# A two-block transformer layer on one core: index projections moved ahead of the convolution's, six taps moved from VectorE to ScalarE, one weight unit split

## The chip, the cores and the metric

One NeuronCore of one Trainium2 chip. The metric is the device time of one execution in microseconds. The profile of this kernel names its engines PE (TensorE, with PEld for its weight loads), DVE (VectorE), ACT (ScalarE), POOL (GpSimd) and SP (SyncE, which issues the loads).

## What is computed

Two transformer blocks on a sequence of 256 tokens and a width of 1024, in fp32. The first is a hybrid layer (three kinds of attention, a 3-tap convolution, a feed-forward part). The change lies in the second block, of which this matters:

```python
n = _rmsnorm(h, norm_mix_g)
z = n @ w_in
c_a, c_g, q, k, v, qi, ki, wi, gc_logit, ga_logit = _split_cols(z, IN_SIZES)
...
u = c_a * sigmoid(c_g)
u = conv31(u) + conv_b                       # 31 taps, causal, each channel by itself
y_conv = silu(_layernorm(u, ln_g, ln_b)) @ w_conv_out
...
logits = einsum('bqhd,bsd->bqhs', qi, ki) * IDX_DIM ** -0.5
score = einsum('bqh,bqhs->bqs', wi, relu(logits))       # causal; the 64 best keys of each query are kept
y_attn = masked_attention(q, k, v, top_k(score)) @ w_attn_out
h = h + (g_conv * y_conv + g_attn * y_attn) @ w_mix_out
```

## The kernel before, in words

**Weight units.** Every projection is cut into units of 512 inputs by 512 outputs (128 x 2048 numbers, 1 MB), 151 in all, in the fixed order of the list `order`; `_pack` lays the weights out in the same order. A unit goes through three steps. SP loads it into one of three buffers `wr`. ACT copies it to `wh`, rounded to the type fp32r (L123), and DVE writes the rest `wr - wh` to `wl` (L126), each as two halves of 128x1024. PE multiplies three times (`mm3`, L263 to L265: high by high, high by low, low by high), 48 matmuls of 256 columns a unit. A unit whose index is in `NATIVE` is not split: PE multiplies the raw fp32 numbers (L292, or L347 where tokens are the output's rows), and neither ACT nor DVE works on it. Three split units can be held (`SPLIT_BUFS`).

**Second block, units 70 to 104.** The input is `xs2` (tiles `xnh`, raw `xn`). The groups come in this order: for half 0 of the channels the convolution's gate `tg` (70, 71) and value `ca` (72, 73); the index queries `qi` (74, 75); the small unit `kiwi` (76); for half 1 `tg` (77, 78) and `ca` (79, 80); then q (81 to 84), k (85 to 88), v (89 to 92), the two gates `gc`, `ga` (93 to 100), and the attention's output product (101 to 104). The evacuation of `ca` makes `u` on DVE (`gated`, L221).

**Side work.** Two generators run beside the groups. At two points in each unit `pump()` lets each go one step, and its instructions stand in the engines' lists from there on.

- `conv()` waits until `u` of a half exists and then applies 31 taps. Tap 0 is four ACT instructions (L1136, with the bias). Of the others, those with `d % 5 < 4` go by ACT: four multiplications into a scratch tile `cp` (L1141), then one addition into `y` over the four channel groups on DVE (L1142). Those with `d % 5 == 4` go by DVE alone, as four multiply-and-add instructions (L1145). `CONV_RATE = (5, 4)` means four pauses for five taps. When both halves are done, DVE sums `y` over the channels (L1152 to L1156) and PE multiplies the sum by ones for the mean (L1159): the start of the layer norm, at whose end the convolution's output product can begin.
- `attention2()` starts when `qi` and `kiwi` exist: index logits on PE (L1060), a ReLU on ACT (L1062), the weighted sum on DVE (L1065), then eight rounds of `max` and `match_replace` on DVE for each half of the queries (L1072, L1073). It goes on with softmax attention once q, k and v are there (L1091 on PE, L1093 to L1103 on DVE and ACT, L1019 and L1032 on PE).

PE's instructions stand in the order of the program. Those of the other engines are ordered once, when the kernel is built. On every engine an instruction runs only after the one ahead of it.

Of the kernel before, what the change touches and what calls it, by code (L numbers as in the profile page):

```python
# [9 lines left out]
F32 = mybir.dt.float32  # L10
F32R = mybir.dt.float32r
AF = mybir.ActivationFunctionType
# [4 lines left out]
T = 256  # L17
# [121 lines left out]

RAW_BUFS = 3  # L140
LOAD_AHEAD = 2
NATIVE = (81, 85, 89, 97)
SPLIT_BUFS = 3
AHEAD = 3
H_BUFS = 24
CONV_RATE = (5, 4)
CONV_ACT = (4, 5)
WARM = 13
LAG = 3
# [11 lines left out]
def hybrid_conformer_kernel(ctx, tc, stop, dbg, xT, memT, wall, wtok, wkiwi, wcmp, par_d, cst_d, gfin_d, out):  # L161
    nc = tc.nc
    V, A, G, P = nc.vector, nc.scalar, nc.gpsimd, nc.tensor
# [4 lines left out]
    psm = ctx.enter_context(tc.tile_pool(name="psm", bufs=4, space=bass.MemoryType.PSUM))  # L168
    pss = ctx.enter_context(tc.tile_pool(name="pss", bufs=3, space=bass.MemoryType.PSUM))
    pso = ctx.enter_context(tc.tile_pool(name="pso", bufs=1, space=bass.MemoryType.PSUM))  # L170

    order = ["main"] * 4 + ["tok"] * 2 + ["main"] * 70 + ["kiwi"] + ["main"] * 74
    for i in NATIVE:
        order[i] = "nat"
    W = Stream(tc, ctx, wall, wtok, wkiwi, order, AHEAD)
# [10 lines left out]
    def H4(dt=F32, name="h"):  # L186
        return half.tile([128, 4, T], dt, name=name, tag="H")

    def S(shape, name, bufs=None, dt=F32):
        return sm.tile(shape, dt, name=name, tag=name, bufs=bufs) if bufs else sm.tile(shape, dt, name=name, tag=name)  # L190
# [20 lines left out]
    def plain(ps):  # L211

        return ps.rearrange("p n (a s) -> p n s a", s=2)

    def v4(ap):
        return ap.rearrange("p n (s a) -> p n s a", s=2)
# [6 lines left out]
    def v3(ap):  # L223
        return ap.rearrange("p (s a) -> p s a", s=2)
# [16 lines left out]
    def pump(n=1):  # L241
        for _ in range(n):
            now = [f for k, f in later if k == 0]
            later[:] = [(k - 1, f) for k, f in later if k]
            for f in now:
                f()
            for g in list(side):
                step(g)
# [5 lines left out]
    def start(gen, urgent=None):  # L254
        side.append((gen, URGENT if urgent is None else urgent))
        return side[-1]

    ALL8 = list(range(8))

    def mm3(ps_ap, wh, wl, xh, xl, first, last):  # L260
        ps_ap = ps_ap.rearrange("p (a s) -> p a s", s=2)
        xh, xl = turns(xh), turns(xl)
        P.matmul(out=ps_ap, lhsT=wh, rhs=xh, start=first, stop=False, skip_group_check=True)  # L263
        P.matmul(out=ps_ap, lhsT=wh, rhs=xl, start=False, stop=False, skip_group_check=True)  # L264
        P.matmul(out=ps_ap, lhsT=wl, rhs=xh, start=False, stop=last, skip_group_check=True)  # L265
# [114 lines left out]
    def group(act, kts, evac, kmajor=False):  # L380
        prod([Feat(act, kts, evac, kmajor)])
# [96 lines left out]
    with tc.manual_schedule(engines=MANUAL):  # L478
# [505 lines left out]
        xs2 = HL("xnh", raws=xn)  # L984
# [142 lines left out]
        def conv():  # L1127
            cnt = 0
            for hf in range(2):
                while ("u", hf) not in done:  # L1130
                    yield
                for d in range(31):
                    w = [par[:, wco + 8 * (30 - d) + 4 * hf + i:wco + 8 * (30 - d) + 4 * hf + i + 1] for i in range(4)]
                    if d == 0:
                        for i in range(4):
                            A.activation(out=y[hf][:, i], in_=u[hf][:, i], func=AF.Identity, scale=w[i],  # L1136
                                         bias=par[:, cbo + 4 * hf + i:cbo + 4 * hf + i + 1])
                    elif d % CONV_ACT[1] < CONV_ACT[0]:
                        p = H4(name="cp")
                        for i in range(4):  # L1140
                            A.activation(out=p[:, i, 0:T - d], in_=u[hf][:, i, 0:T - d], func=AF.Copy, scale=w[i])  # L1141
                        V.tensor_tensor(y[hf][:, :, d:T], y[hf][:, :, d:T], p[:, :, 0:T - d], op=ALU.add)  # L1142
                    else:
                        for i in range(4):
                            V.scalar_tensor_tensor(out=y[hf][:, i, d:T], in0=u[hf][:, i, 0:T - d], scalar=w[i],  # L1145
                                                   in1=y[hf][:, i, d:T], op0=ALU.mult, op1=ALU.add)
                    cnt += 1
                    if cnt * CONV_RATE[1] // CONV_RATE[0] != (cnt - 1) * CONV_RATE[1] // CONV_RATE[0]:
                        yield
                if hf == 0:  # L1150
                    s = H4(name="ys")
                    V.tensor_tensor(s[:, 0:2], y[0][:, 0:2], y[0][:, 2:4], op=ALU.add)  # L1152
                else:
                    V.tensor_tensor(s[:, 2:4], y[1][:, 0:2], y[1][:, 2:4], op=ALU.add)
                    V.tensor_tensor(s[:, 0:2], s[:, 0:2], s[:, 2:4], op=ALU.add)
                    V.tensor_tensor(s[:, 0], s[:, 0], s[:, 1], op=ALU.add)  # L1156
            yield
            ps = PS()
            P.matmul(out=ps[:, 0:T], lhsT=ones, rhs=s[:, 0])  # L1159
            mu = S([128, T], "rb", 4)  # L1160
            V.tensor_scalar(mu, ps[:, 0:T], 1.0 / D, None, op0=ALU.mult)
            sqs = []
            for hf in range(2):
                V.tensor_tensor(y[hf], y[hf], bc(mu, 4), op=ALU.subtract)
                sq = H4(name="sq")
                A.activation(out=sq, in_=y[hf], func=AF.Square)
                sqs.append(sq)
            yield
            var = fold(sqs)
            yield  # L1170
            yield
            ps = col_stats(var)
            yield
            r = rstd_col(ps, D, "rln")
            dg = col_diag(r)
            yield
            ps = diag_bcast(dg)
            rb = S([128, T], "rb", 4)
            A.activation(out=rb, in_=ps, func=AF.Copy)
            for hf in range(2):  # L1180
                t = H4(name="th")
                V.tensor_tensor(y[hf], y[hf], bc(rb, 4), op=ALU.mult)
                for i in range(4):
                    k = 4 * hf + i
                    A.activation(out=at(y, k), in_=at(y, k), func=AF.Identity, scale=par[:, lgo + k:lgo + k + 1],
                                 bias=par[:, lbo + k:lbo + k + 1])
                A.activation(out=t, in_=y[hf], func=AF.Tanh, scale=0.5)
                V.scalar_tensor_tensor(out=y[hf], in0=t, scalar=1.0, in1=y[hf], op0=ALU.add, op1=ALU.mult)
                split_into(ss_, y[hf], 4, 4 * hf, scale=0.5)

        cv = start(conv(), CONV_URGENT)

        for hf in range(2):
            tg = H4(name="tg")

            def ev_cg(ps, o, n):
                A.activation(out=v4(tg[:, o:o + n]), in_=ps, func=AF.Tanh, scale=0.5)

            def ev_ca(ps, o, n):
                gated(u[hf][:, o:o + n], tg[:, o:o + n], ps)  # L1200
                if o == 2:
                    done.add(("u", hf))

            group(xs2, ALL8, ev_cg)
            group(xs2, ALL8, ev_ca)
            if hf == 1:
                break

            qi = H4(name="qi")

            def ev_qi(ps, o, n):
                A.activation(out=v4(qi[:, o:o + n]), in_=ps, func=AF.Copy)

            group(xs2, ALL8, ev_qi)
            kiwi = S([128, T], "rb", 4)
            ps = psm.tile([128, 2, T], F32, name="m", tag="m")
            wh, wl = W.next()
            for k in range(8):
                sl = slice(128 * k, 128 * k + 128)
                mm3(ps[:, 0], wh[:, sl], wl[:, sl], xs2.hi(k), xs2.lo(k), k == 0, k == 7)  # L1220
            A.activation(out=v3(kiwi), in_=plain(ps)[:, 0], func=AF.Copy)
            pump()
            at2 = start(attention2())

        for dst in (q2, k2):
            for hf in range(2):
# [143 lines left out]
        for hf in range(2):  # L1370
            sl = slice(512 * hf, 512 * hf + 512)
# [35 lines left out]
def _units(w, pairs=0):  # L1407

    K, N = w.shape
    g = w.reshape(K // 512, 4, 128, N // 512, 512).transpose(3, 0, 2, 1, 4).reshape(N // 512, K // 512, 128, 2048)  # L1410
    a = g[:2 * pairs].reshape(pairs, 2, K // 512, 128, 2048).transpose(0, 2, 1, 3, 4)
    return np.concatenate([a.reshape(-1, 128, 2048), g[2 * pairs:].reshape(-1, 128, 2048)])
# [12 lines left out]
def _pack(inputs):  # L1425
# [12 lines left out]
    wkv = f["wx_kv_2"][0]  # L1438
    units += [_units(wkv[:, :512])]
    sl = lambda a, n: w2[:, a:a + n]  # L1440
    for h in range(2):
        units += [_units(sl(1024 + 512 * h, 512)), _units(sl(512 * h, 512))]
        if h == 0:
            units += [_units(sl(5120, 512))]
    units += [_units(sl(2048, 2048)), _turned(_units(sl(4096, 1024))), _units(sl(5704, 2048))]
    units += [_units(f["w_attn_out_2"][0]), _units(f["w_conv_out_2"][0], 1), _units(f["w_mix_out_2"][0], 1)]
    xq, xv = _units(f["wx_q_2"][0]), _turned(_units(wkv[:, 512:]))
# [72 lines left out]
```

## Time and profile before

| | |
|---|---|
| median of 3 runs | 895.7 us (895.48 to 896.13) |
| the profiled execution | 895.34 us, its span 893.6 us |
| PE, PEld busy | 881.4, 851.9 us |
| DVE, ACT busy | 659.9, 545.6 us |
| granted TensorE clock | 0.999 |

The span reaches from the first to the last instruction; 1.74 us of the profiled execution lie around it. A busy time is the union of an engine's instructions. Since one matmul begins before the last has ended, PE counts as busy all along while it is fed. In a timeline a row gives start, duration, engine, line, operation, tiles and count, and in brackets the idle time ahead of it with what ended it.

### The profile page before, as it was taken

How to read it: one execution, taken by the hardware profiler on the slowest of the kernel's cores; microseconds unless marked ns; L12 is line 12 of the kernel's file. 1: busy time of each engine (PE TensorE's matmuls, PEld its weight loads, DVE VectorE, ACT ScalarE, POOL GpSimd, SP SyncE). 2: the span in 40 equal slices, each digit the busy share in tenths (PEclk: the TensorE clock that was granted, in tenths of full speed). 3: DMA queues.
4: the chain of work that ended last, by engine and by line, in shares of the span. 5: the costliest groups of instructions: out<-in, count | busy, mean ns of one | idle time of the engine just before them, and what ended most of it. 6: DMA issues, size and time to landing. Idle time of an engine off the chain costs nothing.

```text
span 893.6 us, 17269 instructions
## 1 busy us (share of the span) xinstructions
PE 881.4 (99%) x7240; PEld 851.9 (95%) x7240; DVE 659.9 (74%) x1037; ACT 545.6 (61%) x925; POOL 17.8 (2%) x21
## 2 busy tenths in 40 slices
PE   8999999999999999999999999999999999999996
PEld 8999999999999999999998989999999999998885
DVE  6678899457786675648699999997787777665542
ACT  7634667444575564435697799977566657564432
POOL 0111000000000000000000000000000000000000
PEclk9999999999999999999999999999999999999999
DMA  8844523555555576554553356354665265555541
GB/s 306 313 167 151 211 100 137 170 205 193 189 190 189 194 247 218 191 189 143 193 207 103 138 194 231 124 193 153 208 252 201 95 217 189 191 201 214 192 142 48
DMA packets 25566, 165.01 MB, mean 185 GB/s; under 512 B 2960, under 2 KB 3600, under 8 KB 6928
## 3 DMA queue, kind: packets, MB, share of 16 engines
q1 hardware_dynamic: 25056, 163.37, 51.8%
q8 instruction: 57, 0.93, 0.4%
q10 hardware_dynamic: 432, 0.53, 0.2%
q14 instruction: 21, 0.17, 0.1%
HBM read 162.58 MB, written 1.05 MB: 183 GB/s over the span
## 4 chain that ended last, share of the span: by engine, by line
PE 81%; DVE 11%; ACT 4%; issue 2%; DMA 2%; POOLq 0%; POOL 0%; DVEq 0%; ACTq 0%
PE m L263 22%; PE m L264 22%; PE m L265 21%; PE m L350 3%; PE m L351 3%; PE m L352 3%; DVE wl L126 3%; DVE y L1142 3%; ACT cp L1141 2%; DMA wr<-in_wall_dram 1%; DVE y L1145 1%; ACT wh L123 1%; PE o L780 1%; PE s L764 1%; DVE acc L1073 1%
## 5 line engine op out<-in xcount | busy, mean ns | idle before, releaser
L126 DVE TENSOR_TENSOR wl<-wr,wh 128x1024 fp32r<-128x1024 f32 (+2 forms) x300 | 350.0, 1190 | 155.4 <-ACT wh L123 155.0
L123 ACT ACTIVATE wh<-wr 128x1024 fp32r<-128x1024 f32 (+2 forms) x300 | 298.7, 1029 | 202.6 <-PE m L264 99.6
L263 PE MATMUL m<-xh,wh 128*128 128x256 f32 x384 | 108.3, 282 | 0.6 <-ACT xh L518 0.6
L264 PE MATMUL m<-xh,wh 128*128 128x256 f32 x384 | 106.0, 276 | 0.9 <-DVE xh L520 0.9
L263 PE MATMUL m<-xnh,wh 128*128 128x256 f32 x376 | 106.6, 283 | 0.0
L265 PE MATMUL m<-xh,wl 128*128 128x256 f32 x384 | 105.6, 275 | 0.0
L264 PE MATMUL m<-xnh,wh 128*128 128x256 f32 x376 | 103.4, 275 | 0.0
L265 PE MATMUL m<-xnh,wl 128*128 128x256 f32 x376 | 103.4, 275 | 0.0
L1141 ACT ACTIVATE cp<-u,par 128x255 f32<-128x255 f32 (+23 forms) x192 | 78.8, 490 | 0.0
L263 PEld LDWEIGHTS m<-xh,wh 128*128 128x128 f32 x384 | 73.6, 192 | 2.6 <-issue 1.4
L264 PEld LDWEIGHTS m<-xh,wh 128*128 128x128 f32 x384 | 73.7, 192 | 1.7 <-DVE xh L520 1.7
L265 PEld LDWEIGHTS m<-xh,wl 128*128 128x128 f32 x384 | 73.7, 192 | 0.0
L264 PEld LDWEIGHTS m<-xnh,wh 128*128 128x128 f32 x376 | 72.2, 192 | 0.7 <-issue 0.5
L263 PEld LDWEIGHTS m<-xnh,wh 128*128 128x128 f32 x376 | 72.2, 192 | 0.7 <-issue 0.5
L265 PEld LDWEIGHTS m<-xnh,wl 128*128 128x128 f32 x376 | 72.2, 192 | 0.0
L263 PE MATMUL m<-x5h,wh 128*128 128x256 f32 x256 | 70.8, 277 | 0.0
L263 PE MATMUL m<-fh,wh 128*128 128x256 f32 x256 | 70.6, 276 | 0.0
L263 PE MATMUL m<-hh,wh 128*128 128x256 f32 x256 | 70.6, 276 | 0.0
L265 PE MATMUL m<-x5h,wl 128*128 128x256 f32 x256 | 70.4, 275 | 0.0
L264 PE MATMUL m<-fh,wh 128*128 128x256 f32 x256 | 70.4, 275 | 0.0
L265 PE MATMUL m<-fh,wl 128*128 128x256 f32 x256 | 70.4, 275 | 0.0
L264 PE MATMUL m<-hh,wh 128*128 128x256 f32 x256 | 70.4, 275 | 0.0
(380 smaller groups left out, 2323.0 us busy)
## 6 DMA issues: line engine op xcount, KB each, us to landing
wr<-in_wall_dram SPq DMA_DIRECT2D x145, 1024.0 KB, 4.9
wr<-in_wall_dram SPq DMA_DIRECT2D x4, 512.0 KB, 9.0
mem<-in_memT_dram SPq DMA_DIRECT2D x4, 512.0 KB, 6.0
wr<-in_wtok_dram SPq DMA_DIRECT2D x2, 560.0 KB, 5.1
wr<-in_wall_dram SPq DMA_DIRECT2D x4, 256.0 KB, 4.8
wck<-in_wcmp_dram SPq DMA_DIRECT2D x2, 512.0 KB, 5.9
cst<-in_cst_dram SPq DMA_DIRECT2D x1, 776.0 KB, 10.6
x<-in_xT_dram SPq DMA_DIRECT2D x2, 256.0 KB, 4.3
```

What stands on the lines that cost most here:

```text
L123: self.nc.scalar.activation(out=hi[:, sl], in_=raw[:, sl], func=AF.Copy)
L126: self.nc.vector.tensor_sub(lo[:, sl], raw[:, sl], hi[:, sl].bitcast(F32))
L263: P.matmul(out=ps_ap, lhsT=wh, rhs=xh, start=first, stop=False, skip_group_check=True)
L264: P.matmul(out=ps_ap, lhsT=wh, rhs=xl, start=False, stop=False, skip_group_check=True)
L265: P.matmul(out=ps_ap, lhsT=wl, rhs=xh, start=False, stop=last, skip_group_check=True)
L350: P.matmul(out=o, lhsT=xh, rhs=wh[:, w], start=first, stop=False)
L351: P.matmul(out=o, lhsT=xh, rhs=wl[:, w], start=False, stop=False)
L352: P.matmul(out=o, lhsT=xl, rhs=wh[:, w], start=False, stop=last)
L764: P.transpose(out=psv[:, br, b], in_=pr[:, br, b * 128:b * 128 + 128], identity=ident)
L780: P.matmul(out=po[64 * g:64 * g + 64, 0:128], lhsT=vtok[:, b, c0:c0 + 64], rhs=pts[g][:, br, b], start=False, stop=(br == 1 and b == nb - ...
L1141: A.activation(out=p[:, i, 0:T - d], in_=u[hf][:, i, 0:T - d], func=AF.Copy, scale=w[i])
L1142: V.tensor_tensor(y[hf][:, :, d:T], y[hf][:, :, d:T], p[:, :, 0:T - d], op=ALU.add)
```

## The change

The groups `qi` and `kiwi`, and with them the start of `attention2()`, come ahead of both halves of `tg` and `ca`: `qi` is now units 70 and 71, `kiwi` 72, `tg` and `ca` of half 0 are 73 to 76, those of half 1 stay 77 to 80, and all behind them keeps its place. The list `order` and `_pack` follow. `conv()` is started after `kiwi` rather than before the groups. In half 0 all 30 taps behind tap 0 go by ACT and DVE's addition; in half 1 six still go by DVE alone. `CONV_RATE` becomes (7, 5). Unit 89, the first of v, leaves `NATIVE` and is split like the others.

```diff
--- before.py
+++ after.py
@@ -139,11 +139,11 @@
 
 RAW_BUFS = 3
 LOAD_AHEAD = 2
-NATIVE = (81, 85, 89, 97)
+NATIVE = (81, 85, 97)
 SPLIT_BUFS = 3
 AHEAD = 3
 H_BUFS = 24
-CONV_RATE = (5, 4)
+CONV_RATE = (7, 5)
 CONV_ACT = (4, 5)
 WARM = 13
 LAG = 3
@@ -169,7 +169,7 @@
     pss = ctx.enter_context(tc.tile_pool(name="pss", bufs=3, space=bass.MemoryType.PSUM))
     pso = ctx.enter_context(tc.tile_pool(name="pso", bufs=1, space=bass.MemoryType.PSUM))
 
-    order = ["main"] * 4 + ["tok"] * 2 + ["main"] * 70 + ["kiwi"] + ["main"] * 74
+    order = ["main"] * 4 + ["tok"] * 2 + ["main"] * 66 + ["kiwi"] + ["main"] * 78
     for i in NATIVE:
         order[i] = "nat"
     W = Stream(tc, ctx, wall, wtok, wkiwi, order, AHEAD)
@@ -1135,7 +1135,7 @@
                         for i in range(4):
                             A.activation(out=y[hf][:, i], in_=u[hf][:, i], func=AF.Identity, scale=w[i],
                                          bias=par[:, cbo + 4 * hf + i:cbo + 4 * hf + i + 1])
-                    elif d % CONV_ACT[1] < CONV_ACT[0]:
+                    elif hf == 0 or d % CONV_ACT[1] < CONV_ACT[0]:
                         p = H4(name="cp")
                         for i in range(4):
                             A.activation(out=p[:, i, 0:T - d], in_=u[hf][:, i, 0:T - d], func=AF.Copy, scale=w[i])
@@ -1188,6 +1188,23 @@
                 V.scalar_tensor_tensor(out=y[hf], in0=t, scalar=1.0, in1=y[hf], op0=ALU.add, op1=ALU.mult)
                 split_into(ss_, y[hf], 4, 4 * hf, scale=0.5)
 
+
+        qi = H4(name="qi")
+
+        def ev_qi(ps, o, n):
+            A.activation(out=v4(qi[:, o:o + n]), in_=ps, func=AF.Copy)
+
+        group(xs2, ALL8, ev_qi)
+        kiwi = S([128, T], "rb", 4)
+        ps = psm.tile([128, 2, T], F32, name="m", tag="m")
+        wh, wl = W.next()
+        for k in range(8):
+            sl = slice(128 * k, 128 * k + 128)
+            mm3(ps[:, 0], wh[:, sl], wl[:, sl], xs2.hi(k), xs2.lo(k), k == 0, k == 7)
+        A.activation(out=v3(kiwi), in_=plain(ps)[:, 0], func=AF.Copy)
+        pump()
+        at2 = start(attention2())
+
         cv = start(conv(), CONV_URGENT)
 
         for hf in range(2):
@@ -1203,24 +1220,6 @@
 
             group(xs2, ALL8, ev_cg)
             group(xs2, ALL8, ev_ca)
-            if hf == 1:
-                break
-
-            qi = H4(name="qi")
-
-            def ev_qi(ps, o, n):
-                A.activation(out=v4(qi[:, o:o + n]), in_=ps, func=AF.Copy)
-
-            group(xs2, ALL8, ev_qi)
-            kiwi = S([128, T], "rb", 4)
-            ps = psm.tile([128, 2, T], F32, name="m", tag="m")
-            wh, wl = W.next()
-            for k in range(8):
-                sl = slice(128 * k, 128 * k + 128)
-                mm3(ps[:, 0], wh[:, sl], wl[:, sl], xs2.hi(k), xs2.lo(k), k == 0, k == 7)
-            A.activation(out=v3(kiwi), in_=plain(ps)[:, 0], func=AF.Copy)
-            pump()
-            at2 = start(attention2())
 
         for dst in (q2, k2):
             for hf in range(2):
@@ -1438,10 +1437,9 @@
     wkv = f["wx_kv_2"][0]
     units += [_units(wkv[:, :512])]
     sl = lambda a, n: w2[:, a:a + n]
+    units += [_units(sl(5120, 512))]
     for h in range(2):
         units += [_units(sl(1024 + 512 * h, 512)), _units(sl(512 * h, 512))]
-        if h == 0:
-            units += [_units(sl(5120, 512))]
     units += [_units(sl(2048, 2048)), _turned(_units(sl(4096, 1024))), _units(sl(5704, 2048))]
     units += [_units(f["w_attn_out_2"][0]), _units(f["w_conv_out_2"][0], 1), _units(f["w_mix_out_2"][0], 1)]
     xq, xv = _units(f["wx_q_2"][0]), _turned(_units(wkv[:, 512:]))
```

Three places show how the instructions move. The names: `tg`, `u`, `y`, `cp`, `ys` belong to the convolution; `kid` and `pr` with L1062 to the index; `wh` and `wl` are a unit's two parts; `xnh` the input; `pt`, `ah` and `ga` belong to attention and gates.

ACT's list where the convolution starts, before (from the last split of unit 73 on):

```order
L1197 ACTIVATE tg<-m 128x512
L123 ACTIVATE wh<-wr 128x1024
L1197 ACTIVATE tg<-m 128x512
L123 ACTIVATE wh<-wr 128x1024 x3
L1136 ACTIVATE y<-u,par 128x256 x2
L1141 ACTIVATE cp<-u,par 128x255 x2
L1141 ACTIVATE cp<-u,par 128x254
```

and in the changed kernel:

```order
L1050 ACTIVATE kid<-s 64x256 x2
L123 ACTIVATE wh<-wr 128x1024
L1062 ACTIVATE pr<-s 128x2x128
...
L1062 ACTIVATE pr<-s 128x2x128
L123 ACTIVATE wh<-wr 128x1024 x2
L1062 ACTIVATE pr<-s 128x512 x2
L1136 ACTIVATE y<-u,par 128x256
L1141 ACTIVATE cp<-u,par 128x255
L1141 ACTIVATE cp<-u,par 128x254
```

Tap 0 (L1136) stood ahead of all index work; now `kid` and six of the eight ReLUs stand ahead of it, and the splits up to unit 78.

ACT's list at the convolution's end, before:

```order
L1141 ACTIVATE cp<-u,par 128x226
L1037 ACTIVATE ah<-o 128x2x128
L1141 ACTIVATE cp<-u,par 128x226 x3
L123 ACTIVATE wh<-wr 128x1024
L1021 ACTIVATE pt<-s 128x512
L1244 ACTIVATE ga<-m,par 128x256
L1037 ACTIVATE ah<-s 128x2x128
L1244 ACTIVATE ga<-m,par 128x256
```

and now:

```order
L1141 ACTIVATE cp<-u,par 128x228 x4
L123 ACTIVATE wh<-wr 128x1024 x2
L1021 ACTIVATE pt<-s 128x512
L1243 ACTIVATE ga<-m,par 128x256
L1037 ACTIVATE ah<-o 128x2x128
L1037 ACTIVATE ah<-s 128x2x128
L1243 ACTIVATE ga<-m,par 128x256
L1141 ACTIVATE cp<-u,par 128x226 x4
L1243 ACTIVATE ga<-m,par 128x256 x2
L123 ACTIVATE wh<-wr 128x1024
```

The last tap's multiplications (128x226) stand behind one more `pt` and `ah`; the split behind them is in both the first half of unit 101. From the first L1136 to the last L1141 the list before holds 192 `cp`, 41 halves of splits (units 76 to 100, the small unit counted as one half), 8 ReLUs, 2 `qi`, 1 `kiwi` copy and 2 `kid`; now it holds 216 `cp`, 38 halves (units 79 to 100) and 2 ReLUs.

DVE's list from the last addition to the layer norm, before:

```order
L1142 TENSOR_TENSOR y<-y,cp 128x4x226
L1154 TENSOR_TENSOR ys<-y 128x512
L126 TENSOR_TENSOR wl<-wr,wh 128x1024
L1038 TENSOR_TENSOR ah<-s,ah 128x2x128
L1155 TENSOR_TENSOR ys<-ys 128x512
L1156 TENSOR_TENSOR ys<-ys 128x256
L126 TENSOR_TENSOR wl<-wr,wh 128x1024
```

and now:

```order
L1142 TENSOR_TENSOR y<-y,cp 128x4x226
L126 TENSOR_TENSOR wl<-wr,wh 128x1024
L1038 TENSOR_TENSOR ah<-o,ah 128x2x128
L1154 TENSOR_TENSOR ys<-y 128x512
L126 TENSOR_TENSOR wl<-wr,wh 128x1024
L1155 TENSOR_TENSOR ys<-ys 128x512
L1156 TENSOR_TENSOR ys<-ys 128x256
```

Both halves of unit 101 now stand between the last addition and the sum over channels, where one stood. On PE, L1159 stays where it was, behind the first half of unit 99.

## Rows read from the trace of the kernel before

**Rows 1.** The page: busy us (share of the span) xinstructions of each engine.

```profile
PE 881.4 (99%) x7240; PEld 851.9 (95%) x7240; DVE 659.9 (74%) x1037; ACT 545.6 (61%) x925; POOL 17.8 (2%) x21
```

**Rows 2.** Windows of 10 us: length, PE, PEld, DVE, ACT, POOL busy, clock, DMA share, GB/s.

```profile
470.00:480.00 10.00, 10.00 (x69) 8.41 (x69) 10.00 (x33) 7.65 (x14) 0.00 (x0) 1.00 0.16 47
...
530.00:540.00 10.00, 10.00 (x42) 7.66 (x41) 9.79 (x12) 10.00 (x21) 0.00 (x0) 1.00 0.65 250
```

**Rows 3.** Timeline of PE where the layer norm's first matmul waits.

```profile
597.25 0.28 PE L265 MATMUL m<-xnh,wl 128*128 128x256 f32 x1
598.66 0.67 PE L1159 MATMUL s<-ys,ones 128*128 128x256 f32 x2 [1.14 <-DVE ys L1156]
```

**Rows 4.** Timeline of DVE at the same place, from the last addition on.

```profile
594.17 1.09 DVE L1142 TENSOR_TENSOR y<-y,cp 128x904 f32<-128x904 f32 x1
595.30 0.69 DVE L1154 TENSOR_TENSOR ys<-y 128x512 f32<-128x512 f32 x1
595.91 1.22 DVE L126 TENSOR_TENSOR wl<-wr,wh 128x1024 fp32r<-128x1024 f32 x1
597.04 0.42 DVE L1038 TENSOR_TENSOR ah<-s,ah 128x256 fp32r<-128x256 f32 x1
597.38 0.68 DVE L1155 TENSOR_TENSOR ys<-ys 128x512 f32<-128x512 f32 x1
598.09 0.42 DVE L1156 TENSOR_TENSOR ys<-ys 128x256 f32<-128x256 f32 x1
```

**Rows 5.** Window from tap 0 to ACT's last multiplication; columns as in rows 2.

```profile
437.19:593.02 155.83, 155.07 (x1138) 143.57 (x1137) 148.77 (x264) 144.32 (x323) 0.00 (x0) 1.00 0.46 166
```

**Rows 6.** ACT's longest wait in that window: us in total, times, longest.

```profile
ACT wh L123 <- DMA wr<-in_wall_dram: 5.5, 2, 3.9
```

**Rows 7.** ACT's timeline: starts of neighbours give what each instruction takes.

```profile
437.19 1.09 ACT L1136 ACTIVATE y<-u,par 128x256 f32<-128x256 f32 x2 [1.78 <-DVE u L221]
...
444.98 1.99 ACT L123 ACTIVATE wh<-wr 128x1024 fp32r<-128x1024 f32 x2
446.87 0.61 ACT L1212 ACTIVATE qi<-m 128x512 f32<-128x512 f32 x1
447.37 2.86 ACT L1141 ACTIVATE cp<-u,par 128x251 f32<-128x251 f32 x7
450.13 0.58 ACT L1212 ACTIVATE qi<-m 128x512 f32<-128x512 f32 x1
...
457.02 0.76 ACT L1050 ACTIVATE kid<-s 64x256 f32<-64x256 f32 x2
...
460.08 0.39 ACT L1062 ACTIVATE pr<-s 128x256 f32<-128x256 f32 x1
460.36 1.06 ACT L123 ACTIVATE wh<-wr 128x1024 fp32r<-128x1024 f32 x1
```

**Rows 8.** PE's timeline: unit 70's first matmul, then index matmuls between units.

```profile
417.19 0.28 PE L263 MATMUL m<-xnh,wh 128*128 128x256 f32 x1
...
454.71 0.60 PE L1046 MATMUL s<-rb,cst 128*128 128x256 f32 x2
...
455.51 0.36 PE L263 MATMUL m<-xnh,wh 128*128 128x256 f32 x1
...
458.27 0.60 PE L1060 MATMUL s<-kid,qi 128*128 128x256 f32 x2
458.52 0.46 PE L263 MATMUL m<-xnh,wh 128*128 128x256 f32 x1
```

**Rows 9.** PE's timeline at native unit 89 and the unit behind it.

```profile
525.48 7.03 PE L347 MATMUL m<-wr,xn 128*128 128x512 f32 x16
531.95 0.78 PE L350 MATMUL m<-wh,xnh 128*128 128x512 f32 x1
```

**Rows 10.** DVE by line from 441 to 599 us: count, busy us, mean ns, idle before.

```profile
L1142 DVE TENSOR_TENSOR y<-y,cp 128x1020 f32<-128x1020 f32 (+23 forms) x48 | 55.6, 1159 | 5.0 <-ACT cp L1141 3.7
...
L1145 DVE SCALAR_TENSOR_TENSOR y<-u,par,y 128x252 f32<-128x252 f32 (+5 forms) x48 | 20.4, 463 | 0.0
```

## The prediction

> **What bounds the kernel now.** I read the page first. PE is busy for 99% of the span and its weight loads for 95%; DVE and ACT stand at 74% and 61% [rows 1]. Over the whole kernel this is a TensorE kernel, and a change to the other engines should be nearly free.
>
> The shares are means over stages, so next come the windows of 10 us in the stage that is edited, about 437 to 599 us. There DVE and ACT are nearly full: at 470 us DVE 10.00 of 10 and ACT 7.65, at 530 us 9.79 and 10.00 [rows 2]. PE is still fed, because the splits of its weights stand among the convolution's instructions in both lists.
>
> Third, PE's timeline where the two sides meet. L1159, the layer norm's first matmul, needs every tap of the convolution. PE was done with the matmuls ahead of it at about 597.4 us (the last begins at 597.25, and they begin 0.11 apart), and began L1159 at 598.66, held by DVE's `ys` [rows 3]. This is the place to watch: PE works in order, so whatever makes the convolution later is paid here in full. The convolution was 1.1 us late already.
>
> Fourth, what the convolution's end comes from. DVE's last addition began at 594.17 [rows 4], right behind ACT's last multiplications, which ended at 593.02. From tap 0 at 437.19 to there ACT was busy for 144.32 us and idle for 155.83 - 144.32 = 11.5 us [rows 5]. The longest wait in it was for loads, 5.5 us in two pieces [rows 6]. So ACT has 11.5 us of room in the window, which is what the change uses.
>
> **The change, part by part.** *Order.* PE has the same units up to 80, in another order. It gets later to the place that starts the convolution: half way through the second unit of `ca`, where the first `u` is made. In matmuls from the start of unit 70 that was number 168 (three and a half units of 48), and is now 288 (`qi` 96, the small unit 24, `tg` 96, `ca` 72). From 417.19 to 454.71 PE took 336 matmuls, 0.1117 us each [rows 8]. So the place was at 417.19 + 168 x 0.1117 = 435.95, and tap 0 began 1.24 us behind it, at 437.19 [rows 7]. Now it comes at 417.19 + 288 x 0.1117 = 449.4, plus the index matmuls that have moved ahead of it: the block at 454.71, 0.80 us, and five of L1060, four of 0.25 (458.27 to 458.52) and one of twice the columns, about 0.5 [rows 8]; together 451.7. With the same 1.24 us tap 0 starts at 452.9, **15.7 us later**. Before, ACT used those 15.7 us mostly for the convolution. L1159 does not move on PE, so the start is later and the due time is not.
>
> *ACT's work from tap 0 to the last multiplication.* I start from the 144.3 us of rows 5 and count what the lists hold there, with prices from neighbours in ACT's timeline [rows 7]:
> - 24 more multiplications (six taps, four each): seven take 447.37 to 450.13, 0.394 each; +9.5.
> - Splits: 38 halves for 41. Two of unit 89 come in, those of 76 to 78 now stand ahead. Two halves take 444.98 to 446.87, 0.945 each; -2.8.
> - Two `qi` copies (446.87 to 447.37, 0.5 each), -1.0; the small copy and two `kid` (0.76 for the pair), -1.0.
> - Six of eight ReLUs: four small (460.08 to 460.36, 0.28), two with the columns of a `qi` copy, 0.5; -2.1.
> - One `pt` and one `ah` more stand ahead of the last tap; priced as the large and small ReLU, +0.8.
>
> Sum: 147.7 us. With no idle time at all ACT ends the last tap at 452.9 + 147.7 = **600.6**, against 593.02 before. The room of 11.5 us does not help: it lay inside a window that has lost 15.7 us at its front.
>
> *Idle time of ACT in the new window.* It can be nothing, or as before, 11.5 us. I take nothing: ACT waited before where it ran ahead of PE (an evacuation not yet there) or of the loads, and it is now behind both. The other end counts for the range.
>
> *From ACT's last tap to L1159.* Before: 598.66 - 593.02 = 5.6 us. Now both halves of unit 101 stand on DVE between the last addition and the last sum, and their `wh` stands on ACT behind the last tap. So: two `ga` (about 0.4 each, an estimate from the small multiplications) and one half split on ACT, 0.8 + 0.95; then on DVE `wl` 1.13, `ah` 0.34, `ys` 0.61, `wl` 1.13, `ys` 0.71 and 0.57 to L1159 [rows 4]; 6.2 us. L1159 starts at 600.6 + 6.2 = 606.8, **8.1 us later** than before.
>
> *DVE.* A tap by L1145 cost 4 x 20.4 / 48 = 1.7 us, an addition by L1142 55.6 / 48 = 1.16 [rows 10]. Six taps save 3.2 us, unit 89's `wl` costs 2 x 1.13 [rows 4], and most of the index work moves ahead of the window. DVE gets lighter by the end of the stage; it will wait for `cp`, so this gains nothing.
>
> Here a rule bears on the edit. A tap on ACT costs 4 x 0.394 = 1.6 us there and 1.16 on DVE, against 1.7 on DVE alone. The Trainium skill, "ScalarE: Activation LUTs", section "Rules for kernel authors", says that a plain multiplication belongs on VectorE, not ScalarE. With the six taps left on DVE the sum for ACT would be 138.2 and L1159 would come at 597.3, 1.4 us earlier than before.
>
> *Unit 89.* The native unit took 531.95 - 525.48 = 6.5 us [rows 9], a split unit takes 48 x 0.1117 = 5.4. PE saves 1.1 us ahead of L1159 and then waits for it; the gain is hidden by the wait. If there were no wait, it would show in full.
>
> *Loads.* SP issues the same loads; the small one is four places earlier. A split unit's buffer is free when DVE has made `wl`, and ACT's splits now come later than before, not earlier, than the loads. Nothing.
>
> *Behind L1159.* The work on PE up to the end is the same, and the layer norm follows L1159 as before (DVE has one `wl` less ahead of the mean). I carry the 8.1 us through to the end. Against the profiled execution, 895.34 us (a span of 893.6 and 1.74 around it): 895.34 + 8.1 = **903.4 us**. The median of the runs, 895.7, is 0.4 higher, within what they spread by (0.65); I leave the forecast at 903.4.
>
> **The rivals.** About 0.2%, 1.8 us, is what a measurement can tell from no change.
>
> *A. ACT has the room; PE decides (faster).* Decides if ACT's window shrinks to where the last tap ends before 597.4 - 1.1 - 6.2 = 590.1, which needs 10.5 us less work than I count. For it: the 11.5 us of idle time, and PE's 95%. Against: the two counted starts and the lists. Then the native unit's 1.1 us and the wait of 1.1 us are gained: 893.1 us. The Trainium skill, "Perfetto Trace Analysis", section "Identifying the Most-Contended Engine", has one judge TensorE by its weight loads' busy share and optimize the engine with the highest share first; by that, with 95%, the time would follow PE's work, as in A. The stage's windows speak otherwise: ACT 10.00 at 530 us.
>
> *B. ACT also waits (slower still).* The 5.5 us for loads [rows 6] return, since a unit's load waits for a `wl` that now waits for a later `wh`: 895.34 + 8.1 + 5.5 = 909 us; with all 11.5 us it would be 915. Against: ACT gets to each split later than the load.
>
> *C. The multiplications get cheaper.* With long rows of them and a lighter DVE, 0.02 us less on each of 216 is 4.3 us (the size is a guess, a twentieth): 899 us. Against: the seven of rows 7 were back to back already.
>
> *D. No change.* A and the forecast meet half way, ACT ending about 593: 895 us. That the change does not do what it says is excluded by the lists.
>
> **How the numbers follow.** Forecast 0.62 (901.5 to 906.5: the start and tail uncertain by 1 us, a little idle time), B 0.16, C 0.08, A 0.10, D 0.04. The likeliest gives 903.4. The range reaches from 899.5 (half of C) to 909 (half of B), leaving out A, D and the outer halves. Faster 0.10, same 0.04, slower 0.86.
>
> **What would show it.** Tap 0 on ACT at about 453; ACT without gaps from there to about 600; L1159 waiting some 9 us for `ys`, at about 607; DVE with gaps that end at `cp`; a tail from L1159 to the end as long as before, 295 us. I am wrong if ACT shows gaps of 5 us or more in that window and L1159 comes on time, or if the loss stands somewhere else on PE, at the splits of units 90 to 100 or behind L1159.

## The result, and the profile after

The change makes the kernel slower: 908.45 us median (907.09 to 909.95) against 895.75 us, a ratio of 1.0142 with the interval 1.012 to 1.0164. The profiled execution took 909.77 us, with a span of 908.0 us against 893.6; the other three took 909.95, 907.14 and 907.09 us.

The page shows almost nothing of it; PE's share fell by one point [rows 1]:

```profile
PE 886.6 (98%) x7248; PEld 859.2 (95%) x7248; DVE 662.2 (73%) x1021; ACT 556.8 (61%) x951; POOL 17.8 (2%) x21
```

PE's timeline around L1159, as in [rows 3]. PE has nothing to do for 5.96 us, and then something new: the next matmuls begin 0.21 us apart instead of 0.11, until 616.1. The 24 matmuls of the half unit behind L1159 take 611.70 to 616.74, 5.0 us.

```profile
604.47 0.61 PE L1032 MATMUL o<-pt,v 128*128 128x128 f32 x4
611.04 1.22 PE L1159 MATMUL s<-ys,ones 128*128 128x256 f32 x2 [5.96 <-DVE ys L1156]
611.70 0.78 PE L263 MATMUL m<-xnh,wh 128*128 128x256 f32 x1
612.26 0.42 PE L264 MATMUL m<-xnh,wh 128*128 128x256 f32 x1
612.48 0.42 PE L265 MATMUL m<-xnh,wl 128*128 128x256 f32 x1
...
616.63 0.28 PE L265 MATMUL m<-xnh,wl 128*128 128x256 f32 x1
616.74 1.06 PE L1032 MATMUL s<-pt,v 128*128 128x128 f32 x8
```

Before, the same 24 matmuls took 2.76 us:

```profile
599.53 0.36 PE L263 MATMUL m<-xnh,wh 128*128 128x256 f32 x1
...
602.29 1.06 PE L1032 MATMUL s<-pt,v 128*128 128x128 f32 x8
```

Windows of 2 us at the same place (the columns of [rows 2]; the clock is the number behind POOL). The granted clock falls inside the idle time, between 608 and 610 us (a mean of 0.86), and is 0.50, 1.2 instead of 2.4 GHz, from there to about 616 us:

```profile
606.00:608.00 2.00, 0.00 (x0) 0.00 (x0) 2.00 (x3) 1.81 (x3) 0.00 (x0) 1.00 0.50 102
608.00:610.00 2.00, 0.00 (x0) 0.00 (x0) 2.00 (x4) 0.00 (x0) 0.00 (x0) 0.86 1.00 422
610.00:612.00 2.00, 0.96 (x3) 0.84 (x3) 0.95 (x2) 0.00 (x0) 0.00 (x0) 0.50 0.51 102
612.00:614.00 2.00, 2.00 (x11) 1.95 (x10) 1.67 (x3) 0.00 (x0) 0.00 (x0) 0.50 0.95 401
614.00:616.00 2.00, 2.00 (x11) 2.00 (x11) 1.81 (x2) 1.85 (x2) 0.00 (x0) 0.50 0.05 21
616.00:618.00 2.00, 2.00 (x19) 2.00 (x19) 1.39 (x2) 1.44 (x3) 0.00 (x0) 0.93 0.00 0
```

The window from tap 0 to the end of the last multiplication, as in [rows 5]. ACT is idle for 0.4 us instead of 11.5:

```profile
457.78:604.79 147.01, 142.47 (x1041) 133.74 (x1041) 137.53 (x214) 146.61 (x335) 0.00 (x0) 0.99 0.45 158
```

ACT's timeline at its two ends [rows 7], tap 0 and the last tap:

```profile
457.78 0.60 ACT L1136 ACTIVATE y<-u,par 128x256 f32<-128x256 f32 x1 [1.40 <-DVE u L221]
...
603.29 1.63 ACT L1141 ACTIVATE cp<-u,par 128x226 f32<-128x226 f32 x4
604.79 0.86 ACT L1243 ACTIVATE ga<-m,par 128x256 f32<-128x256 f32 x2
```

DVE from there to L1159 [rows 4]. Both halves of a split (L126) stand between the last addition and the last sum:

```profile
605.59 1.10 DVE L1142 TENSOR_TENSOR y<-y,cp 128x904 f32<-128x904 f32 x1
606.62 1.23 DVE L126 TENSOR_TENSOR wl<-wr,wh 128x1024 fp32r<-128x1024 f32 x1
607.77 0.42 DVE L1038 TENSOR_TENSOR ah<-o,ah 128x256 fp32r<-128x256 f32 x1
608.10 0.68 DVE L1154 TENSOR_TENSOR ys<-y 128x512 f32<-128x512 f32 x1
608.70 1.22 DVE L126 TENSOR_TENSOR wl<-wr,wh 128x1024 fp32r<-128x1024 f32 x1
609.84 0.69 DVE L1155 TENSOR_TENSOR ys<-ys 128x512 f32<-128x512 f32 x1
610.56 0.42 DVE L1156 TENSOR_TENSOR ys<-ys 128x256 f32<-128x256 f32 x1
```

PE's waits: line, what for, us in total, times, longest. Before, the first was 1.1 us, that for `xh` 0.6, and of the others there was none; between unit 70 and L1159 PE had one more wait, of 0.7 us at L1019.

```profile
PE s L1159 <- DVE ys L1156: 6.0, 1, 6.0
PE m L265 <- DVE wl L126: 2.3, 4, 1.5
PE m L263 <- ACT xh L518: 1.9, 1, 1.9
...
PE m L351 <- DVE wl L126: 1.0, 1, 1.0
PE m L350 <- ACT wh L123: 0.8, 1, 0.8
```

The 14.4 us between the spans divide by three marks on PE (unit 70's first matmul, L1159, the end of the span):

| Stretch | before | after | more | forecast |
|---|---|---|---|---|
| to unit 70 | 417.19 | 419.10 | 1.9 | 0 |
| unit 70 to L1159 | 181.47 | 191.94 | 10.5 | 8.1 |
| L1159 to the end | 294.90 | 296.95 | 2.0 | 0 |

The 1.9 us ahead of unit 70 are not the change's. They stand in the first 17 us: PE waits 1.9 us for the first activations (`xh` L518, above) instead of 0.6, and behind it the clock reads 0.53 (12 to 14 us) and 0.62 (14 to 16 us), where it was 1.00 before. Unit 70 starts at 416.9 to 419.1 us in the traces of all the kernels below, whose program is the same up to there.

Of the 10.5 us, the wait at L1159 itself has grown by only 4.8 (from 1.14 to 5.96). PE comes to L1159 at 605.08, which is 5.6 us later than before, counted from unit 70, although unit 89 takes 5.2 us instead of 6.5: it waits 4.1 us at the splits of units 91 to 96 (L350, L351 and L265 above).

### The profile page after: what moved, and what is told of

It reads as the page before. It is cut to its first block, busy times and chain, and to the rows that moved or that the text cites. A ratio compares the mean times of both kernels' runs of the same rounds, so it can differ in the third digit from the quotient of the medians.

```text
span 908.0 us, 17305 instructions
## 1 busy us (share of the span) xinstructions
PE 886.6 (98%) x7248; PEld 859.2 (95%) x7248; DVE 662.2 (73%) x1021; ACT 556.8 (61%) x951; POOL 17.8 (2%) x21
## 4 chain that ended last, share of the span: by engine, by line
PE 78%; ACT 13%; DVE 5%; issue 2%; DMA 1%; SPq 0%; POOLq 0%; POOL 0%; DVEq 0%; ACTq 0%
PE m L263 21%; PE m L264 21%; PE m L265 21%; ACT cp L1141 7%; ACT wh L123 4%; PE m L350 3%; PE m L351 3%; PE m L352 3%; DVE wl L126 2%; DVE y L1142 1%; DMA wr<-in_wall_dram 1%; ACT pr L1099 1%; PE o L780 1%; PE s L764 1%; ACT pt L1021 0%
## 5 line engine op out<-in xcount | busy, mean ns | idle before, releaser
L126 DVE TENSOR_TENSOR wl<-wr,wh 128x1024 fp32r<-128x1024 f32 (+2 forms) x302 | 352.6, 1189 | 160.3 <-ACT wh L123 159.9
L263 PE MATMUL m<-xnh,wh 128*128 128x256 f32 x376 | 108.7, 289 | 0.0
L265 PE MATMUL m<-xnh,wl 128*128 128x256 f32 x376 | 104.7, 278 | 2.3 <-DVE wl L126 2.3
L265 PE MATMUL m<-xh,wl 128*128 128x256 f32 x384 | 106.4, 277 | 0.0
L264 PE MATMUL m<-xnh,wh 128*128 128x256 f32 x376 | 104.4, 278 | 0.0
L1141 ACT ACTIVATE cp<-u,par 128x255 f32<-128x255 f32 (+29 forms) x216 | 88.4, 529 | 0.0
L265 PEld LDWEIGHTS m<-xnh,wl 128*128 128x128 f32 x376 | 73.1, 194 | 3.1 <-DVE wl L126 3.1
L265 PEld LDWEIGHTS m<-xh,wl 128*128 128x128 f32 x384 | 74.5, 194 | 0.0
L264 PEld LDWEIGHTS m<-xnh,wh 128*128 128x128 f32 x376 | 73.2, 195 | 1.3 <-issue 1.0
L263 PEld LDWEIGHTS m<-xnh,wh 128*128 128x128 f32 x376 | 73.1, 195 | 1.3 <-issue 0.7
L265 PE MATMUL m<-fh,wl 128*128 128x256 f32 x256 | 70.4, 275 | 0.0
L265 PE MATMUL m<-hh,wl 128*128 128x256 f32 x256 | 70.4, 275 | 0.0
```

The costliest lines, as they stand in the source:

```text
L126: self.nc.vector.tensor_sub(lo[:, sl], raw[:, sl], hi[:, sl].bitcast(F32))
```

## The experiments

One part at a time first, undone or done alone. Ratios are to the kernel before. Theory 1 was that ScalarE's added work makes the loss, theory 2 that the convolution's later start does.

**e1: the six taps back on VectorE** (in the changed kernel).

```diff
-                    elif hf == 0 or d % CONV_ACT[1] < CONV_ACT[0]:
+                    elif d % CONV_ACT[1] < CONV_ACT[0]:
```

> The changed kernel with the taps of half 0 shared as before (24 of 30 by ScalarE). Theory 1 (ScalarE's work between tap 0 and the last tap, from a later start, sets when L1159 runs): 24 multiplications of 0.39 us leave ScalarE, so L1159 comes 9.5 us earlier than in the changed kernel, and the wait at L1159 with the low clock behind it all but vanishes: 895 to 898 us. Theory 2 (the later start itself costs, whatever ScalarE then has to do): 904 us or more.

905.64 us, ratio 1.0106 [1.0091, 1.0121]. Theory 1 falls. ACT has less work, but now it waits for loads:

```profile
ACT wh L123 <- DMA wr<-in_wall_dram: 6.6, 3, 2.8
```

**e2: the six taps alone** (in the kernel before; the same line the other way).

> The kernel before, with the taps of half 0 all by ScalarE and nothing else. Theory 1: 9.5 us more on ScalarE, of which its 11.5 us of idle time in the window take a part, since some of that idle time stands where it waits for TensorE: the last tap 2 to 8 us later, 898 to 904 us. If idle time took it all: 895 us (the loss then needs the new order). If it took none: 905 us or more.

895.46 us, ratio 0.9998 [0.9988, 1.0007]: free. ACT's idle time was room for them (busy 153.5 us of 155.9 from tap 0 to the last multiplication), as long as the start did not move.

**e3: unit 89 native again** (in the changed kernel: `NATIVE = (81, 85, 89, 97)`).

> The changed kernel with unit 89 native again. Theory 1: 1.9 us less on ScalarE in the window, hence L1159 1.9 us earlier and 905.5 to 907 us; TensorE's 1.1 us more are hidden by the wait. Theory 3 (TensorE's own work decides): 1.1 us slower than the changed kernel, 909.5 us.

905.54 us, ratio 1.0106 [1.0091, 1.0121]. L1159 still waits 5.7 us, but the waits at splits fall from 4.1 us to 0.5. The split of unit 89 costs some 3 us here, where ACT has no room for it (busy 143.84 us of 143.84 from tap 0 to its last multiplication even without it).

**e4: the new order alone** (in the kernel before: the moved projections with their weights; taps, rate and native units as they were).

> The kernel before with the index projections moved ahead and nothing else: taps, rate and native units as before. Theory 1: tap 0 starts at 456 us, ScalarE's work is 147.7 - 9.5 - 1.9 = 136.3 us, the last tap ends at 592 to 593 as before: 894.5 to 897 us. Theory 2: the later start costs by itself, 900 us or more.

904.5 us (902.26 to 904.65), ratio 1.009 [1.0075, 1.0105]. The order alone costs two thirds of what the change does; theory 2 holds. At the old rate L1159 stands later on PE and waits only 2.1 us, but PE then runs out of other work ahead of the matmuls on `sh`, the layer norm's result:

```profile
PE m L263 <- ACT sh L394: 5.0, 1, 5.0
PE s L1159 <- DVE ys L1156: 2.1, 1, 2.1
```

**e5: L1159 later on PE.** Two more `yield`s in the changed kernel. In the trace 56 more matmuls stand ahead of L1159, some 6.2 us by their prices (48 at 0.1117 us and eight of L1032 in 0.81), rather than the 76 and 8.6 us that were expected.

```diff
             yield
+            yield
+            yield
             ps = PS()
             P.matmul(out=ps[:, 0:T], lhsT=ones, rhs=s[:, 0])
```

> The changed kernel, with two yields more ahead of L1159, which moves that matmul some 76 matmuls (76 x 0.1125 us = 8.6 us) later in TensorE's order; nothing else moves. In the changed kernel TensorE comes to L1159 at 605.0 us and stands still for 6.0 us, then runs 24 matmuls at the low clock (2.0 us lost). Theory 1 (the place of L1159 in TensorE's order turns a late convolution into loss; the rest of the chain has 6 us of slack ahead of `sh`): no wait at L1159, no fall of the clock after it, TensorE reaches the matmuls on `sh` some 8 us earlier and waits there for 1 to 2 us: 901 to 903. Theory 2 (the chain of the convolution itself is the bound, wherever TensorE meets it): the same 8 us stand at `sh`: 906 to 909.

901.28 us, ratio 1.0057 [1.0042, 1.0072]: 7.2 us come back from two lines that change no work. L1159 (now L1161) waits 1.15 us, the clock stays at 1.00, and `sh` is there in time (ready at 635.2, used at 637.2). The place of L1159 is thus more than half of the loss: 4.8 us less wait and 2.3 us from the 24 matmuls at full clock. The rest stands at splits, 5.5 us of waits:

```profile
PE m L265 <- DVE wl L126: 3.1, 4, 1.5
PE m L351 <- DVE wl L126: 1.6, 2, 1.0
...
PE s L1161 <- DVE ys L1156: 1.1, 1, 1.1
...
PE m L350 <- ACT wh L123: 0.8, 1, 0.8
```

**e6: the old rate in the changed kernel** (`CONV_RATE = (5, 4)`).

> The changed kernel with the convolution paced as before (5 steps per 4 yields instead of 7 per 5); L1159 then stands 124 matmuls (14 us) later in TensorE's order, and each step of the convolution is given out later too. Theory 1 (place of L1159 alone): no wait at L1159, but the chain behind it (24 to 25 us to the first `sh`) then ends 5 us behind TensorE: 902 to 906, with a wait of about 5 us at `sh` as in the run with the order alone. Rival (the faster pace of the changed kernel is itself what costs, by crowding VectorE and ScalarE with splits waiting): below 900.

907.31 us, ratio 1.0124 [1.0109, 1.0139], over the upper end of what was expected. L1159 stands later, but the taps are given out later as well: the last multiplication starts at 608.4 us (604.4 in the changed kernel), so L1159 waits 4.6 us after all, and `sh` 5.0.

**e7: less work.** Taps 19 to 30 of the first half are left out of the computation.

```diff
+                    elif hf == 0 and d > 18:
+                        pass
                     elif hf == 0 or d % CONV_ACT[1] < CONV_ACT[0]:
```

> The changed kernel without taps 19 to 30 of the first half (left out of the computation); the yields between steps stay. ScalarE does 12 x 4 x 0.39 = 18.7 us less, VectorE 12 x 1.15 = 13.8 us less. Theory 1 (the later start costs because the convolution's work no longer fits between its start and L1159): the last tap ends some 14 to 18 us earlier, TensorE waits nowhere at L1159 and not at splits: 893 to 896. Rival (the new order costs somewhere else: the attention's indices, the loads, the splits): stays at 900 or above.

899.65 us, ratio 1.0036 [1.0022, 1.0051]: between the two theories, and the most useful miss. The waits at splits are gone, but L1159 still waits:

```profile
PE s L1161 <- DVE ys L1158: 4.8, 1, 4.8
```

Counted from unit 70, the last multiplication starts 9.7 us earlier than in the changed kernel, not 18.7. ACT, with less to do, is idle again (137.30 - 128.27 = 9.0 us):

```profile
457.67:594.97 137.30, 137.30 (x1027) 130.68 (x1026) 123.76 (x201) 128.27 (x285) 0.00 (x0) 1.00 0.47 169
```

So the end of the convolution is not start plus ACT's work alone. The taps are given out step by step with PE's groups and queue behind evacuations and splits that wait for PE or a load: in this window ACT waits 4.8 us for loads and 4.2 us for PE. In the program the last tap stands two pauses ahead of L1159, with fewer taps as with all. Its addition, the splits and the sums take 6.6 us from the end of the last multiplication (595.13) to L1161 (601.72), and PE is there after 1.8.

**e8: all but the order** (the kernel before with taps, rate and native units of the change).

> The kernel before with three of the four parts: first half's taps all on ScalarE, rate 7 to 5, units 81, 85 and 97 native; the index projections stay between the halves. Tap 0 starts at 437.2 again. Theory 1 (the order alone costs): 147 to 150 us of ScalarE work and 6.2 us of tail put the sum `ys` at 590.4 to 593.4; L1159 stands 71 matmuls (8 us) earlier in TensorE's order than before, at 589.6: a wait of 1 to 4 us, 894 to 898. Rival (the four taps more on ScalarE, or the pace, cost by themselves what the change costs): 903 or more.

917.6 us, ratio 1.0237 [1.0222, 1.0253], far beyond theory 1, and slower than the whole change. **e10** asks which part it was: the kernel before with `CONV_RATE = (7, 5)` alone.

> The kernel before with the rate 7 to 5 alone; taps, order and native units as before. L1159 stands 94 matmuls (some 10 us) earlier in TensorE's order, at about 587. Theory 1a (the faster pace is what cost in the run without the order: more of the convolution stands ahead of the splits in the queues of VectorE and ScalarE, and L1159 comes before its sum): TensorE waits at L1159 for 5 to 9 us and for splits for some us: 901 to 912. Rival (the four taps more on ScalarE and the split of unit 89 cost there, the pace is harmless): 896 to 899, with a wait of 1 to 3 us.

913.66 us, ratio 1.0197 [1.0183, 1.0211]. Most of it is the rate, 17.8 of 21.7 us; the rest was not divided between taps and unit 89. L1159 now stands ahead of the last two fp32 groups on PE (L292): PE reaches it 15 us earlier than before, at 582.3, while `ys` is done at 593.7, only 4.9 us earlier. The wait is followed by 5 us at the low clock (0.50 up to 598, 0.67 from 598 to 600 us):

```profile
593.72 1.22 PE L1159 MATMUL s<-ys,ones 128*128 128x256 f32 x2 [11.41 <-DVE ys L1156]
...
596.44 1.06 PE L1019 MATMUL s<-cst,pr 128*128 128x128 f32 x4
597.29 1.92 PE L1032 MATMUL s<-pt,v 128*128 128x128 f32 x8
599.00 3.77 PE L292 MATMUL m<-xn,wr 128*128 128x256 f32 x16
```

The four products of L1019 take 596.44 to 597.29, 0.85 us, against 0.41 to 0.44 in the kernel before. Rate and order thus belong together: the rate is there to put L1159 back where it was after the start has moved by 18.7 us, and each alone costs 8 to 18 us.

**e11: order and rate, with e1's, e3's and e5's edits.**

> The changed kernel with unit 89 native again, taps 4 and 5 of each five back on VectorE, and two yields more ahead of L1159: what is left is the new order and the rate. The two parts took 2.8 and 2.9 us away each by itself, the yields 7.2: theory 1 (they add up, the loss is work that no longer fits before L1159): 908.4 - 12.9 = 895.5, so 895 to 898. Rival (the order has a cost of its own, by the later end of the chain at `sh`): 899 to 902, with a wait of 2 us or more at `sh` or L1161.

898.03 us (896.76 to 899.91), ratio 1.0022 [1.0013, 1.0031]; no wait at L1161 (`ys` done at 604.6, PE there at 606.8), none at `sh`, the clock at 1.00. Together the three edits bring 10.4 us, less than the 12.9 that they bring singly, and about 2 us remain with the new order and rate. PE now waits in attention instead, for ScalarE's `pt`, where the kernel before waited 0.7 us at L1019:

```profile
PE s L1019 <- ACT pt L1021: 2.7, 2, 1.9
```

**e9 and e12: can the kernel before be beaten?** e9 is the kernel before with e5's two yields, e12 that with unit 89 split as well.

> The kernel before with two yields more ahead of L1159, which moves it 53 matmuls (6 us) later in TensorE's order. Theory 1 (the place of L1159 costs what TensorE waits there): the 1.1 us of wait goes, and the chain behind it, which has 6.4 us of slack ahead of the matmuls on `sh`, loses most of that slack: 894.3 to 895.3. Rival (the same wait stands at `sh`, or the chain comes late there): 895.5 to 898.

> The kernel before with unit 89 split instead of native and two yields more ahead of L1159. TensorE's own work falls by 1.1 us, ScalarE and VectorE get 2 us and 2.4 us of split work. Theory 1 (before, the split is covered by ScalarE's 11.5 us of idle time): 893.2 to 894.6, faster than the kernel before by 1 to 2 us. Rival (VectorE has no room for it: it comes late at splits of units 89 to 100): 895 to 898.

e9: 895.21 us, ratio 0.9989 [0.998, 0.9998], the fastest of all, though by less than the 0.2% that count as a difference here. The wait of 1.1 us is gone. e12: 895.42 us, ratio 1.0001 [0.999, 1.0013]. The 1.1 us that PE saves on unit 89 are given back: PE waits for `pr` on DVE, which is full at that place (10.00 of 10 us from 570 to 580, as is ACT); in e9 this wait is 0.6 us.

```profile
PE s L1019 <- DVE pr L1093: 2.3, 2, 1.4
```

## Why the prediction was right, and where it was not

The sign was right, and so was most of the mechanism: a convolution that starts later and a matmul on PE that does not move. Forecast 903.4 us in 899.5 to 909, measured 908.45. That this lies in the range is partly luck. It is outside 901.5 to 906.5, which was meant for the forecast's own mechanism, and inside only by the room left for rival B, whose loads did not come back. Point by point:

- *Tap 0, 15.7 us later.* Measured from unit 70: 38.7 us instead of 20.0, so 18.7 later. The term was short by 3.0 us. 1.1 us is PE. The pairs of L1060 were priced rightly (0.25 us, and 0.46 for the wide one), but the matmul behind a pair is slow too: the next begins 0.29 us behind it after a narrow pair and 0.51 after the wide one, as below, where 0.11 is usual. 1.9 us is DVE: the forecast carried over the lag of 1.24 us of before, but `u` now queues behind a split and the search for the 64 best keys, which moved ahead as well:

```profile
451.18 1.02 PE L1060 MATMUL s<-kid,qi 128*128 128x512 f32 x2
451.64 0.67 PE L263 MATMUL m<-xnh,wh 128*128 128x256 f32 x1
452.15 0.28 PE L264 MATMUL m<-xnh,wh 128*128 128x256 f32 x1
...
455.95 1.21 DVE L126 TENSOR_TENSOR wl<-wr,wh 128x1024 fp32r<-128x1024 f32 x1
457.07 0.08 DVE L1073 MATCH_VALUE_LOAD acc<-m,acc 128x8 f32 x1
457.14 0.28 DVE L1073 MATCH_REPLACE8 acc<-m,acc 128x128 f32<-128x128 f32 x1
457.33 0.41 DVE L221 SCALAR_TENSOR_TENSOR u<-tg,m 128x256 f32<-128x256 f32 x1
```

- *ACT's work, 147.7 us without idle time.* 146.6 us of work in 147.0. The number held, the model behind it only half: e1 and e7 show that taking ACT's work away gives back only part of it (L1159 2.5 us earlier for 9.5 in e1, the last tap 9.7 for 18.7 in e7, counted from unit 70), because ACT then waits. The sentence weighed beside it, that with the six taps on DVE L1159 would come at 597.3, some 10 us earlier, falls with e1: L1159 came at 606.5 us there, and the whole kernel gained 2.8. The Trainium skill's rule that a plain multiplication belongs on VectorE ("ScalarE: Activation LUTs", section "Rules for kernel authors") was thus worth 2.8 us in the new order, and in the old one nothing (e2).
- *Tail of 6.2 us from the last multiplication to L1159.* 611.04 - 604.79 = 6.25.
- *Unit 89's gain is hidden by the wait.* It was, and splitting it cost 2.9 us (e3), of which the forecast had 1.9 in ACT's sum (two halves of 0.945). That DVE has no room for it at its fullest place either, the step on DVE left out; e12 shows it without the wait at L1159.
- *Loads: nothing.* Held; in the window ACT waits for none, where it waited 5.5 us before [rows 6].
- *PE up to L1159, unmoved, with a wait of some 9 us.* This step failed, though L1159 started no later for it: the wait was 6.0 us, because PE itself came 5.6 us later. The waits at the splits of units 91 to 96, 4.1 us, are among the signs of being wrong that the prediction named. In the changed kernel they lie within the time that `ys` takes anyway; with L1159 moved they are most of what is left (e5).
- *Behind L1159, nothing.* This step failed as well, by 2.0 us: the 24 matmuls behind L1159 took 5.0 us instead of 2.76, at half the clock. It was not in the trace of before, where PE waited 1.1 us and the clock stayed.
- *Rivals.* A (PE decides, 893.1) is out: PE's weight loads are at 95% in both kernels and 12.7 us were lost, so the trace does not agree with choosing by the highest share. B's loads did not return. C: a multiplication of the same width takes the same (128x226: 0.374 us from start to start in both traces); the whole sum came out 0.7 us lower, not 4.3, with the later taps narrower than the one that was priced. D is out by the interval.

In short, 3.0 us at tap 0, 2.0 us of clock and 1.9 us at the start of the profiled run, less 0.7 in ACT's sum, take the forecast of 903.4 to 909.6, against the profiled 909.77.

## What to carry to other kernels

In a kernel whose order is written by pumping side work between matmul groups, a matmul that consumes the side work has a fixed place in TensorE's list; a change that starts the side work later, or gives it out at another rate, moves due time and finish time apart, and TensorE, which works through its list in order, pays the difference. Before moving anything, read from the trace when each such matmul is reached and when its operand is done, and move the consumer (here two `yield`s, 7.2 us) before touching the work. That helps only as far as the chain behind it has room: in e4 and e6, where the convolution ended later as well, PE waited 5.0 us at `sh`. Taking work off an engine that shows 10.00 of 10 gave back only part of it here, where the work is handed out step by step.

## What was not expected of the hardware

A wait of TensorE can cost more than its length. Behind waits of 4.6 to 11.4 us at L1159 the granted clock was 0.50 (1.2 GHz) for some 3.5 to 6 us; behind the 2.1 us of e4 for some 3.4:

```profile
614.00:616.00 2.00, 2.00 (x11) 1.93 (x10) 2.00 (x3) 0.00 (x0) 0.00 (x0) 0.52 0.90 381
616.00:618.00 2.00, 2.00 (x13) 2.00 (x13) 2.00 (x3) 0.73 (x1) 0.00 (x0) 0.62 0.44 94
```

Behind the 1.1 us of before and of e5 it was not. In the changed kernel two waits of 0.80 and 0.95 us close together, at 538 to 540 us, were followed by it too:

```profile
538.00:540.00 2.00, 0.48 (x1) 0.19 (x1) 2.00 (x2) 2.00 (x4) 0.00 (x0) 1.00 0.00 0
540.00:542.00 2.00, 1.85 (x7) 1.56 (x8) 2.00 (x5) 2.00 (x7) 0.00 (x0) 0.79 0.00 0
542.00:544.00 2.00, 2.00 (x6) 1.61 (x5) 1.90 (x4) 2.00 (x4) 0.00 (x0) 0.50 0.80 233
```

In e5, though, the same two waits (0.82 and 0.96 us, between 537.1 and 539.4 us) were not; the clock stayed at 1.00:

```profile
542.00:544.00 2.00, 2.00 (x11) 1.76 (x10) 1.90 (x3) 2.00 (x4) 0.00 (x0) 1.00 0.83 336
```

So the length of the waits alone does not tell, and no run here shows what does. The fall at 541 us cost the changed kernel nothing in the end: counted from unit 70, PE began the next matmul that a split held up in both (L265) at 133.66 us there and at 133.69 in e5, which had waited 1.4 us more at splits up to that point.
